# One pass over the first gate/up products, with the first product copied from bank to bank

## The chip, the cores and the metric

The kernel runs on one core of a Trainium2 chip. The core has TensorE (PE in the profile: matmuls, with the load of the stationary operand, PEld, beside them), VectorE (DVE), ScalarE (ACT), GpSimd (POOL) and SyncE (SP, which here only issues DMAs). On-chip memory is SBUF, 128 partitions wide; TensorE writes its sums to PSUM, which has eight banks of 128 x 512 float32. The metric is the device time of one execution, in microseconds, as a median of several runs. Less is better.

## The reference

One decoder layer on 2048 tokens of width 1024, all in float32:

```python
hn = rms_norm(h, mix_pre_g)
proj = hn @ w_in                                   # q, k, v and the convolution group's input u
attn_out = sliding_window_attention(q, k, v, attn_sinks, rel_bias)   # window 128
conv_out = conformer_conv(u, ...)                  # GLU, 31 taps, LayerNorm, swish, @ w_conv_pw
mixed = jnp.concatenate([attn_out, conv_out], axis=-1) @ w_out
h = h + rms_norm(mixed, mix_post_g)
hn = rms_norm(h, ffn_pre_g)
ff = (jax.nn.silu(hn @ w_gate) * (hn @ w_up)) @ w_down               # inner width 2816
h = h + rms_norm(ff, ffn_post_g)
```

## The kernel before

**Number format.** Each float32 operand of a large matmul is split into a high part (rounded to the fp32r format, a ScalarE copy) and a low part (the difference, by VectorE or GpSimd). A product takes three matmuls: high x high, high x low, low x high. One matmul covers 128 x 128 weights by 512 columns.

**Stages.** Tokens go in four tiles of 512 (t or w = 0 to 3). The letter behind the @ in a tile's name in the profile is its stage.

- A (`stage_a`): the first norm and the input projection, 14 units for each token tile. B (`stage_b`): attention in four blocks of 128 tokens. It transposes through the PSUM banks `tr` and has GpSimd mask the probabilities (line 504).
- C: the convolution. `stage_taps` does the 31 taps on VectorE; `stage_tail` (line 578) turns the result through the PSUM bank `ct`, normalises it and writes it to `mixT` in device memory.
- J (`stage_join`, lines 621 to 650): multiplies `w_conv_pw` into the lower half of `w_out` once, so that the convolution's last projection and the output projection become one. Four raw pieces of `w_out` are split into a right operand, two raw pieces of `w_pw` into left operands; the raw tile `wx` has one buffer. The results are written to `w_join`.
- W (`stage_w`, lines 714 to 762): the output projection of one token tile, from `mixT`, in four groups of two inputs; then norm and residual (`norm_w`); `hn` is written to `hn_scr` in device memory.
- H: reads columns of `hn_scr`, transposes them (`turned`, line 828) and splits them into operands of the gate/up matmuls. `stage_h_plain` (line 846) makes B11 and B21, the operands of the token tile `ws[0]`; `stage_h_sums` (line 859) makes the rest.
- F: gate and up. Two token tiles are done together, first (0, 1) and then (2, 3), with a scheme that forms a 2 x 2 block product from seven block products of sums in place of eight. A "matrix" m below is one pair of 128-wide gate or up blocks; there are 22. One block product, `product` (line 896), is 12 matmuls into one bank.
- G (`stage_p2`): the down projection by the same scheme, and the last norm (`finish`).

**The first gate/up stage.** `stage_pre` (lines 904 to 975) does two of the block products ahead of the rest, for the first 20 matrices of tiles (0, 1) and the first 16 of tiles (2, 3): A11 x B11 ("first") and A12 x B21 ("second"), which add up to one block. It runs over q: first all the first products, then all the second ones. A first product is copied by ScalarE from its bank to a `fa` tile (line 965) and written to `keeps` in device memory (line 966). For a second product that sum is read back into one of two `gb` tiles (`fetch`, line 926) and copied by ScalarE into a bank (`seed`, line 941), onto which the second product adds up. Gate results then go through Silu (line 970), up results are multiplied in, and the block is written to `mids`. `stage_p1`, which does the remaining five products of each matrix, reads `keeps` once more (line 1025, seed at line 1054). For matrices that were not done ahead it copies the first product from bank to bank itself (line 1062).

**Order of the work.** The program is written as a main sequence of generators and lanes beside it (`Lane`, lines 1297 to 1344). Each `yield` carries a cost; the main sequence advances a clock, and each lane emits work as its rate allows, if its condition holds. `until` emits the rest of a lane at once. The order of emission sets priorities, and a list scheduler with a simulated time line sets from them the final order on every engine and DMA queue. Engines work strictly in that order. The conditions that matter here:

```python
lh.add(n + ".0", stage_h_plain(ws, ops, n, off), lambda: since(lw, "W0", NH))      # B11, then B21
lw.add("W0", ..., lambda: "A3" in started and "C0" in ld.done)                     # line 1388
ld.add("J", stage_join(), lambda: "A2" in started)                                 # then C0, C1
```

**Buffers.** PSUM has four banks `mm` (products), three `tr` (attention, transposes) and one `ct`. Of the SBUF tiles named here there are four `fa`, two `gb`, eight `hl`, four `mid`, two `mb`, one `wx`, three `fc`. B11 and B21 of tiles (0, 1) lie in `x` and `hl`, those of tiles (2, 3) in `ql` and `mid`; the `mid` tiles are until then those in which the output projection of token tile 3 is summed and normalised.

Of the kernel before, what the change touches and what calls it, by code (L numbers as in the profile page):

```python
# [17 lines left out]
AF = mybir.ActivationFunctionType  # L18
# [7 lines left out]
P = 128  # L26
T = 512
# [10 lines left out]
def layer_kernel(ctx, tc, x, xT, cols, rows, sinks, relb, onehot, w_in, w_pw, w_out, w_gate, w_up, w_down, out):  # L38
    nc = tc.nc
# [7 lines left out]
    lab = ["X0"]  # L47
# [7 lines left out]
    def t_(tag, shape, dt=F32):  # L55
        return sb.tile(list(shape), dt, tag=tag, name=nm(tag), bufs=BUFS[tag])

    def f4(tag, shape=(P, D)):
        return t_(tag, shape)
# [14 lines left out]
    mm = lambda: bank("mm", 4)  # L74
    tr = lambda: bank("tr", 3)
# [517 lines left out]
    def conv_tail(t, yt):  # L593
# [14 lines left out]
        for c in range(4):  # L608
# [9 lines left out]
            yield 2  # L618
            lab[0] = L

    def stage_join():
        lab[0] = "J0"
        right = []
        for k in range(4):
            raw = f4("wx", (P, 2, T))
            nc.sync.dma_start(raw, w_out[4 + k].rearrange("p (a b) -> p a b", a=2))
            yield JL
            for n in range(2):
                lab[0] = "J0"
                right.append(split_w(raw[:, n], "mid" if k < 2 else "chl"))  # L630
            yield 1.5
            lab[0] = "J0"
        for mp in range(2):
            pair_ = t_("yt", (P, 2, 2, T), F32R)
            raw = f4("wx", (P, 2, T))
            nc.sync.dma_start(raw, w_pw[2 * mp : 2 * mp + 2].rearrange("m p t -> p m t"))
            yield JL
            lab[0] = "J0"
            left = [split_w(raw[:, m], pair_[:, m]).rearrange("p a (k c) -> p a k c", c=P) for m in range(2)]
            yield 2  # L640
            for m in range(2):
                for n in range(2):
                    lab[0] = "J0"
                    o = ct()
                    three(o, [((left[m][:, 0, k], left[m][:, 1, k]), (right[2 * k + n][:, 0], right[2 * k + n][:, 1])) for k in range(4)])
                    z = f2("fa")
                    act(z, o, AF.Copy, scale=0.5)
                    nc.scalar.dma_start(w_join[2 * mp + m, :, n * T : (n + 1) * T], z)
                    yield 4
                    lab[0] = "J0"  # L650
# [63 lines left out]
    def stage_w(w, spill, G, atag, htag, mtag, bank_of, norm=None):  # L714
        L = f"W{w}"
        lab[0] = L
        acc = [f4(atag) for _ in range(4)]

        def acts(gi, ms=None):
            aa = []  # L720
            for m in ms or load(gi):
                a = hl(htag)
                act(a[:, 0], m, AF.Copy)  # L723
                vtt(a[:, 1], m, a[:, 0].bitcast(F32), ALU.subtract)
                aa.append([a])
            return aa

        stage = t_("mb", (P, 2, T)) if w == 1 else None

        def load(gi):  # L730
            ms = []
            for c in range(G * gi, G * gi + G):
                ms.append(stage[:, c % 2] if w == 1 else f2(mtag))
                nc.sync.dma_start(ms[-1], mixT[c, :, w * T : (w + 1) * T])
            return ms

        first = load(0)
        gb = load_gb(0) if w > 1 else None
        if w != 1:
            yield 5.0 if w == 0 else 8.0  # L740
            lab[0] = L
        nxt = acts(0, first)
        for gi in range(KC // G):
            aa = nxt
            for n in range(2):
                lab[0] = L
                if n == 0 and gi + 1 < KC // G:
                    if w == 1 and G * gi + G == 4:
                        ld.until("C1")
                        lab[0] = L  # L750
                    rows_next = load(gi + 1)
                if n == 1 and gi + 1 < KC // G:
                    nxt = acts(gi + 1, rows_next)
                src = w_out[2 * gi : 2 * gi + 2] if gi < 2 else w_join[2 * gi - 4 : 2 * gi - 2]
                ws = weight(src[:, :, n * T : (n + 1) * T].rearrange("c p t -> p c t"),
                            lo_out[n, 2 * gi : 2 * gi + 2], w > 0)
                yield from block_half(acc, list(zip(aa, ws)), n, gi == 0, L, bank_of)
        tail = norm_w(w, spill, acc, mtag, gb)
        if norm:
            norm(tail)  # L760
        else:
            yield from tail
# [83 lines left out]
    def stage_h_plain(ws, ops, n, off):  # L846
        L = f"H{ws[0]}"
        for k in range(4):
            lab[0] = L
            b = turned(ws[0], k + off, tr, COLTAG[ws[0]][k] if ws[0] else "fa")  # L850
            u = f2("gb")
            act(u, b, AF.Copy, scale=g_ffn[:, k + off : k + off + 1])
            nc.scalar.dma_start(hT[ws[0] // 2][k + off], u)
            o = op_tile(ws, ops, n, k, {})
            act(o[:, 0], u, AF.Copy)
            lo(u, o, False)
            yield 2.0
# [43 lines left out]
                mat(o, w[:, a, ks], op[k][:, b], start=first and n == 0, stop=n == 11, skip_group_check=not first)  # L901
                n += 1

    def stage_pre(ws, ops, mid, keep, q0=0, q1=None):
        PRE = PRES[ws[0]]
        q1 = q1 or 2 * PRE
        L = f"F{ws[0]}"
        raws = {}
        wops = {}
        kept = {}  # L910

        def load(q):
            if q < q1 and q % 2 == 0:
                lab[0] = L
                half, m = divmod(q, PRE)
                raw = t_("raw", (P, 2, T))
                for j in range(2):
                    src, pr = MATS[m + j]
                    nc.sync.dma_start(raw[:, j], src[2 * pr][:, half * T : (half + 1) * T])
                    raws[q + j] = raw[:, j]  # L920

        def fetch(q):
            if PRE <= q <= q1:
                lab[0] = L
                kept[q] = f2("gb")
                nc.sync.dma_start(kept[q], keep[q - PRE if q < q1 else 0])

        def split(q):
            if q < q1:
                lab[0] = L  # L930
                raw = raws.pop(q)
                wops[q] = split_f(raw, hl("w"))
                lo(raw, wops[q], ws[0] and q % 2 == 1)

        seeded = {}

        def seed(q):
            if PRE <= q < q1:
                lab[0] = L
                seeded[q] = mm()  # L940
                act(seeded[q], kept.pop(q), AF.Copy)  # L941

        load(q0)
        load(q0 + 2)
        for q in range(q0, q0 + 3):
            split(q)
        for q in range(q0, q1):
            half, m = divmod(q, PRE)
            started.add(f"P{ws[0]}.{q}")
            bn = "B21" if half else "B11"  # L950
            if len(ops.get(bn, ())) < 4:
                lh.until(f"{bn}.{ws[0]}")
            split(q + 3)
            load(q + 4)
            if q + 2 == PRE:
                fetch(q + 2)
            lab[0] = L
            seed(q + 1)
            fetch(q + 3)
            lab[0] = L  # L960
            o = seeded.pop(q) if half else mm()
            product(o, wops.pop(q), ops[bn], not half)
            if not half:
                u = f2("fa")
                act(u, o, AF.Copy)
                nc.scalar.dma_start(keep[m], u)
            else:
                if MATS[m][0] is w_gate:
                    sg = f2("fa")
                    act(sg, o, AF.Silu)  # L970
                else:
                    vtt(sg, sg, o, ALU.mult)
                    nc.sync.dma_start(mid[0, MATS[m][1]], sg)
            yield 2.76
        early[ws[0]] = kept.pop(q1)

    early = {}

# [318 lines left out]
    class Lane:  # L1297
# [36 lines left out]
        def until(self, name):  # L1334
            while name not in self.done:
                assert self.items, name
                n, gen, needs = self.items[0]
                assert not needs or needs(), n
                inlane[0] = True
                for c in gen:  # L1340
                    assert c is not None
                inlane[0] = False
                self.done[n] = clk[0]
                self.items.pop(0)

# [10 lines left out]
    NS = 12  # L1356
    AHEAD = 3
    PRES = {0: 20, 2: 16}
    POOL_LO = (3, 6)
    PRE_S0, PRE_S2 = 22, 16  # L1360
    H1, H2, H3, H4 = 0, 4, 7, 11
    NH = 24
    JL = 10
    lb = Lane(RB, 0)
    lc = Lane(RC0, LC)
    lw = Lane(RW0, 0)
# [18 lines left out]
            started.add(name)  # L1385

    lb.add("X", stage_x(), lambda: "x1" in started)
    lw.add("W0", stage_w(0, True, 2, "x", "hl", "fa", mm), lambda: "A3" in started and "C0" in ld.done)
    TGA = [["hl"] * 8, ["mid"] * 4 + ["chl"] * 4, ["hl"] * 8, ["mid"] * 4 + ["hl"] * 4]
    xa = {}  # L1390
    warm = mm()
# [136 lines left out]
```

## Time and profile before

| | |
|---|---|
| median of 3 runs | 1991.51 us (1990.13 to 1993.91) |
| profiled execution | 1997.53 us, span of its instructions 1995.6 us |
| mean granted TensorE clock | 0.989 |
| PE busy | 1940.2 us (97%), 8730 matmuls |
| DVE, ACT, POOL busy | 1488.0 (75%), 970.8 (49%), 331.1 us (17%) |
| device memory | 330.08 MB read, 121.12 MB written, 226 GB/s over the span |

How to read the lines shown below: a line of the waits has the waiting engine, line and tile, what it waited for, then total us, times and longest. A line of a stretch has its bounds, its length and the busy time of PE, PEld, DVE, ACT and POOL with their counts, then the granted clock, the share of the DMA engines and GB/s. A line of a group has line, engine, operation, output and inputs, shape and count, then busy us and mean ns of one, then the idle time ahead of them by what ended it. A line of the time line has start and length in us, engine, line, operation, tiles and count; idle time before it and its releaser stand in brackets. SPq and ACTq are issues of DMAs. A DMA line has line or tiles, count, KB of each, and median us from issue to landing.

### The profile page before, as it was taken

To read this page: it belongs to the slowest core of one execution; us is meant where nothing else is said; L and a number is where in the kernel's file an instruction comes from. 1 tells how busy PE (TensorE), PEld (TensorE's weight loads), DVE (VectorE), ACT (ScalarE), POOL (GpSimd) and SP (SyncE) were. 2 spreads that over 40 slices of the span, in tenths; PEclk is the share of its full clock that TensorE was granted. 3 is DMA by queue.
4 is the path that set the end of the run, shared out by engine and by line. 5 is a ranking of instruction groups with operands and counts; after the bars stand their busy time and mean duration, and the time that the engine had idled before them with its cause. 6 is when DMAs were issued, how large, how long until landed. Compare 5 with 4: busy or idle time off the path is not lost.

```text
span 1995.6 us, 26899 instructions
## 1 busy us (share of the span) xinstructions
PE 1940.2 (97%) x8730; PEld 1546.2 (77%) x8730; DVE 1488.0 (75%) x2679; ACT 970.8 (49%) x1910; POOL 331.1 (17%) x395
## 2 busy tenths in 40 slices
PE   8999999899999999999999999999899999999998
PEld 6877677667777788878878878778688888888886
DVE  5998989955884899988759985675866665555557
ACT  5355334456566643333355446476544333345443
POOL 6001311231111300000000020003523332311000
PEclk9999999999999999999999999999999999999999
DMA  8786654567859876787477687689834442366654
GB/s 311 256 310 217 219 167 143 186 214 253 276 176 332 298 253 239 233 278 260 162 266 245 231 280 270 195 303 353 307 139 169 169 153 101 126 220 212 211 185 159
DMA packets 234364, 452.99 MB, mean 227 GB/s; under 512 B 23496, under 2 KB 49264, under 8 KB 234224
## 3 DMA queue, kind: packets, MB, share of 16 engines
q1 hardware_dynamic: 212592, 415.63, 61.8%
q10 hardware_dynamic: 19392, 28.32, 3.9%
q0 software_dynamic: 2240, 7.34, 1.0%
q8 instruction: 68, 1.11, 0.2%
q14 instruction: 72, 0.59, 0.1%
HBM read 330.08 MB, written 121.12 MB: 226 GB/s over the span
## 4 chain that ended last, share of the span: by engine, by line
PE 76%; DMA 9%; DVE 8%; issue 3%; ACT 3%; POOL 1%; SPq 0%; ACTq 0%; DVEq 0%; POOLq 0%
PE mm@F L108 30%; PE mm@G L108 18%; PE mm@A L108 14%; PE mm@W L108 4%; PE tr@W L108 4%; PE tr@B L108 3%; DMA gb@F<-keeps 2%; DVE fc@C L85 1%; PE ct@J L108 1%; DVE mid@W L85 1%; DMA mixT<-fc@C 1%; DVE w@F L85 1%; DMA chl@F<-w_up 1%; DVE fa@F L85 1%; DVE chl@F L85 1%
## 5 line engine op out<-in xcount | busy, mean ns | idle before, releaser
L85 DVE SCALAR_TENSOR_TENSOR fc@C<-glu@C,colt,fc@C 128x512 f32<-128x512 f32 x480 | 367.9, 782 | 2.4
L108 PE MATMUL mm@F<-hl@H,w@F 128*128 128x512 f32 x1056 | 254.2, 390 | 4.3 <-ACT mm@F L941 4.3
L108 PE MATMUL mm@G<-hl@G,hl@G 128*128 128x512 f32 x924 | 227.4, 397 | 7.4 <-ACT mm@G L1232 2.9
L108 PEld LDWEIGHTS mm@F<-hl@H,w@F 128*128 128x128 f32 x1056 | 197.5, 188 | 47.0 <-ACT mm@F L941 6.2
L108 PE MATMUL mm@A<-hl@A,w@A 128*128 128x512 f32 x840 | 209.4, 398 | 2.6 <-DVE hl@A L85 1.3
L108 PEld LDWEIGHTS mm@G<-hl@G,hl@G 128*128 128x128 f32 x924 | 173.5, 190 | 46.5 <-ACT mm@G L1232 3.4
L108 PE MATMUL mm@G<-w@G,hl@G 128*128 128x512 f32 x876 | 199.7, 389 | 0.0
L814 ACT ACTIVATE w@F<-chl@F 128x512 fp32r<-128x512 f32 x220 | 135.0, 624 | 118.6 <-PE mm@F L108 112.8
L108 PEld LDWEIGHTS mm@G<-w@G,hl@G 128*128 128x128 f32 x876 | 164.3, 188 | 34.4 <-issue 0.3
L108 PEld LDWEIGHTS mm@A<-hl@A,w@A 128*128 128x128 f32 x840 | 156.8, 190 | 40.6 <-DVE hl@A L85 3.0
L85 DVE TENSOR_TENSOR w@F<-chl@F,w@F 128x512 fp32r<-128x512 f32 x198 | 145.2, 735 | 39.0 <-ACT w@F L814 38.8
L108 PE MATMUL mm@F<-mid@H,w@F 128*128 128x512 f32 x528 | 132.3, 394 | 7.9 <-ACT mm@F L941 7.3
L108 PE MATMUL mm@F<-p@H,w@F 128*128 128x512 f32 x528 | 130.6, 393 | 0.0
L108 PE MATMUL mm@F<-ql@H,w@F 128*128 128x512 f32 x528 | 127.1, 390 | 2.0 <-ACT w@F L814 2.0
L108 PE MATMUL mm@F<-x@H,w@F 128*128 128x512 f32 x528 | 126.8, 391 | 1.0 <-DVE x@H L85 0.9
L108 PEld LDWEIGHTS mm@F<-mid@H,w@F 128*128 128x128 f32 x528 | 98.1, 188 | 31.4 <-ACT mm@F L941 9.6
L108 PEld LDWEIGHTS mm@F<-ql@H,w@F 128*128 128x128 f32 x528 | 98.9, 188 | 23.0 <-ACT w@F L814 2.6
L108 PEld LDWEIGHTS mm@F<-p@H,w@F 128*128 128x128 f32 x528 | 100.1, 190 | 21.3 <-ACT at@F L1068 0.4
L108 PEld LDWEIGHTS mm@F<-x@H,w@F 128*128 128x128 f32 x528 | 98.3, 188 | 23.4 <-DVE x@H L85 1.4
L108 PE MATMUL mm@W<-w@W,hl@W 128*128 128x512 f32 x384 | 106.0, 415 | 7.4 <-ACT hl@W L723 5.6
L133 ACT ACTIVATE w@A<-raw@A 128x512 fp32r<-128x512 f32 x110 | 67.4, 626 | 73.9 <-PE mm@A L108 46.1
L85 DVE TENSOR_TENSOR w@G<-raw@G,w@G 128x512 fp32r<-128x512 f32 x73 | 51.2, 701 | 67.6 <-ACT w@G L814 66.6
(301 smaller groups left out, 3307.6 us busy)
## 6 DMA issues: line engine op xcount, KB each, us to landing
mids<-fa@F SPq DMA_DIRECT2D x154, 256.0 KB, 2.7
raw@A<-w_in SPq DMA_DIRECT2D x55, 512.0 KB, 4.4
w@A<-lo_in SPq DMA_DIRECT2D x84, 256.0 KB, 3.4
fc@G<-mids SPq DMA_DIRECT2D x77, 256.0 KB, 3.3
fa@G<-mids SPq DMA_DIRECT2D x75, 256.0 KB, 4.8
gb@F<-keeps SPq DMA_DIRECT2D x74, 256.0 KB, 4.5
w@W<-lo_out SPq DMA_DIRECT2D x48, 256.0 KB, 4.2
chl@F<-w_gate SPq DMA_DIRECT2D x22, 512.0 KB, 3.9
```

What stands on the lines that cost most here:

```text
L85: r = op(*args, **kw)
L108: r = nc.tensor.matmul(*args, **kw)
L133: act(w[:, 0], raw, AF.Copy)
L814: act(w[:, 0], x, AF.Copy)
```

## The change

In `stage_pre` the order becomes pairs of matrices: m first, m+1 first, m second, m+1 second. Behind each first product, after the copy to `fa` and the write to `keeps`, which stay, ScalarE copies the bank into the next `mm` bank, and the second product adds up there. The reads of `keeps` in this stage go, but for one ahead of `stage_p1`. (The new `TWO` would leave so many matrices in the old order; it is 0 for both.) The fetch of that last one is now issued at two steps, the third and the second from the end.

The join has a second raw tile, `spare_tile()`, an `mb` tile that the output projection of token tile 1 uses later in place of its own; loads are issued two ahead, with a pause `JS` of 2 in place of `JL` of 10 behind each. W0 waits for the join in place of the convolution tail C0, and emits the rest of C0 itself ahead of its third group if that is not done. The transposes of `stage_h_plain` for token tile 0 go through `ct` in place of `tr`.

```diff
 def stage_join():
+    srcs = [w_out[4 + k].rearrange("p (a b) -> p a b", a=2) for k in range(4)]
+    srcs += [w_pw[2 * m : 2 * m + 2].rearrange("m p t -> p m t") for m in range(2)]
+    def load(i):
+        if i < len(srcs):
+            raws[i] = spare_tile() if i % 2 else f4("wx", (P, 2, T))
+            nc.sync.dma_start(raws[i], srcs[i])
+    load(0)
+    load(1)
+    yield JL
     for k in range(4):
-        raw = f4("wx", (P, 2, T))
-        nc.sync.dma_start(raw, w_out[4 + k].rearrange("p (a b) -> p a b", a=2))
-        yield JL
         for n in range(2):
-            right.append(split_w(raw[:, n], "mid" if k < 2 else "chl"))
-        yield 1.5
+            right.append(split_w(raws[k][:, n], "mid" if k < 2 else "chl"))
+        yield JS
+        load(k + 2)
+        yield JS
...
-    stage = t_("mb", (P, 2, T)) if w == 1 else None
+    stage = spare_tile() if w == 1 else None
...
-                if w == 1 and G * gi + G == 4:
-                    ld.until("C1")
+                if w < 2 and G * gi + G == 4:
+                    ld.until(f"C{w}")
...
-        b = turned(ws[0], k + off, tr, COLTAG[ws[0]][k] if ws[0] else "fa")
+        b = turned(ws[0], k + off, tr if ws[0] else ct, COLTAG[ws[0]][k] if ws[0] else "fa")
...
-def stage_pre(ws, ops, mid, keep, q0=0, q1=None):
+def stage_pre(ws, ops, mid, keep):
+    PRE, two = PRES[ws[0]], TWO[ws[0]]
+    seq = [(m, half) for half in range(2) for m in range(two)]
+    for m in range(two, PRE, 2):
+        seq += [(m + j, half) for half in range(2) for j in range(2)]
...
+    def stored(q):
+        return q == len(seq) or q < len(seq) and seq[q][1] and seq[q][0] < two
     def fetch(q):
-        if PRE <= q <= q1:
+        if stored(q):
             kept[q] = f2("gb")
-            nc.sync.dma_start(kept[q], keep[q - PRE if q < q1 else 0])
+            nc.sync.dma_start(kept[q], keep[seq[q][0] if q < len(seq) else 0])
...
-    for q in range(q0, q1):
-        half, m = divmod(q, PRE)
+    for q, (m, half) in enumerate(seq):
         bn = "B21" if half else "B11"
         if len(ops.get(bn, ())) < 4:
             lh.until(f"{bn}.{ws[0]}")
         split(q + 3)
         load(q + 4)
-        if q + 2 == PRE:
+        if stored(q + 2) and not stored(q + 1):
             fetch(q + 2)
         seed(q + 1)
         fetch(q + 3)
-        o = seeded.pop(q) if half else mm()
+        o = seeded.pop(m) if half else mm()
         product(o, wops.pop(q), ops[bn], not half)
         if not half:
             u = f2("fa")
             act(u, o, AF.Copy)
             nc.scalar.dma_start(keep[m], u)
+            if m >= two:
+                seeded[m] = mm()
+                act(seeded[m], o, AF.Copy)
...
+TWO = {0: 0, 2: 0}
-JL = 10
+JL, JS = 10, 2
...
-lw.add("W0", ..., lambda: "A3" in started and "C0" in ld.done)
+lw.add("W0", ..., lambda: "A3" in started and "J" in ld.done)
```

More of the change, by code (lines that the diff above doesn't have):

```diff
@@ L619, in conv_tail, with spare_tile @@
             lab[0] = L
+    spare = []
+    def spare_tile():
+        if not spare:
+            spare.append(t_("mb", (P, 2, T)))
+        return spare[0]
     def stage_join():
         lab[0] = "J0"
+        srcs = [w_out[4 + k].rearrange("p (a b) -> p a b", a=2) for k in range(4)]
+        srcs += [w_pw[2 * m : 2 * m + 2].rearrange("m p t -> p m t") for m in range(2)]
+        raws = {}
+        def load(i):
+            if i < len(srcs):
+                lab[0] = "J0"
+                raws[i] = spare_tile() if i % 2 else f4("wx", (P, 2, T))
[3 more added lines that the diff above has]
+        yield JL
         right = []
         for k in range(4):
-            raw = f4("wx", (P, 2, T))
-            nc.sync.dma_start(raw, w_out[4 + k].rearrange("p (a b) -> p a b", a=2))
-            yield JL
             for n in range(2):
                 lab[0] = "J0"
-                right.append(split_w(raw[:, n], "mid" if k < 2 else "chl"))
-            yield 1.5
+                right.append(split_w(raws[k][:, n], "mid" if k < 2 else "chl"))
+            yield JS
+            load(k + 2)
+            yield JS
+        for mp in range(2):
             lab[0] = "J0"
-        for mp in range(2):
             pair_ = t_("yt", (P, 2, 2, T), F32R)
[L635 to L639, printed above, removed]
+            left = [split_w(raws[4 + mp][:, m], pair_[:, m]).rearrange("p a (k c) -> p a k c", c=P) for m in range(2)]
             yield 2
@@ L902, in product @@
                 n += 1
-    def stage_pre(ws, ops, mid, keep, q0=0, q1=None):
-        PRE = PRES[ws[0]]
-        q1 = q1 or 2 * PRE
+    def stage_pre(ws, ops, mid, keep):
+        PRE, two = PRES[ws[0]], TWO[ws[0]]
         L = f"F{ws[0]}"
-        raws = {}
-        wops = {}
-        kept = {}
+        seq = [(m, half) for half in range(2) for m in range(two)]
+        for m in range(two, PRE, 2):
+            seq += [(m + j, half) for half in range(2) for j in range(2)]
+        raws, wops, kept, seeded = {}, {}, {}, {}
         def load(q):
-            if q < q1 and q % 2 == 0:
+            if q < len(seq) and q % 2 == 0:
                 lab[0] = L
-                half, m = divmod(q, PRE)
+                m, half = seq[q]
                 raw = t_("raw", (P, 2, T))
@@ L920, in load @@
                     raws[q + j] = raw[:, j]
+        def stored(q):
+            return q == len(seq) or q < len(seq) and seq[q][1] and seq[q][0] < two
         def fetch(q):
-            if PRE <= q <= q1:
+            if stored(q):
                 lab[0] = L
                 kept[q] = f2("gb")
-                nc.sync.dma_start(kept[q], keep[q - PRE if q < q1 else 0])
+                nc.sync.dma_start(kept[q], keep[seq[q][0] if q < len(seq) else 0])
         def split(q):
-            if q < q1:
+            if q < len(seq):
                 lab[0] = L
@@ L933, in split @@
                 lo(raw, wops[q], ws[0] and q % 2 == 1)
-        seeded = {}
         def seed(q):
-            if PRE <= q < q1:
+            if q < len(seq) and stored(q):
                 lab[0] = L
[L940 to L945, printed above, removed]
+                seeded[seq[q][0]] = mm()
+                act(seeded[seq[q][0]], kept.pop(q), AF.Copy)
+        load(0)
+        load(2)
+        for q in range(3):
             split(q)
-        for q in range(q0, q1):
-            half, m = divmod(q, PRE)
+        for q, (m, half) in enumerate(seq):
             started.add(f"P{ws[0]}.{q}")
@@ L954, in stage_pre @@
             load(q + 4)
-            if q + 2 == PRE:
+            if stored(q + 2) and not stored(q + 1):
                 fetch(q + 2)
-            lab[0] = L
             seed(q + 1)
@@ L974, in stage_pre @@
             yield 2.76
-        early[ws[0]] = kept.pop(q1)
+        early[ws[0]] = kept.pop(len(seq))
     early = {}
@@ L1338, in until @@
                 assert not needs or needs(), n
+                was = inlane[0]
                 inlane[0] = True
@@ L1341, in until @@
                     assert c is not None
-                inlane[0] = False
+                inlane[0] = was
                 self.done[n] = clk[0]
@@ L1387, in layer_kernel @@
     lb.add("X", stage_x(), lambda: "x1" in started)
-    lw.add("W0", stage_w(0, True, 2, "x", "hl", "fa", mm), lambda: "A3" in started and "C0" in ld.done)
+    lw.add("W0", stage_w(0, True, 2, "x", "hl", "fa", mm), lambda: "A3" in started and "J" in ld.done)
     TGA = [["hl"] * 8, ["mid"] * 4 + ["chl"] * 4, ["hl"] * 8, ["mid"] * 4 + ["hl"] * 4]
```

## The prediction

> **What bounds the kernel now.** I read the page first (busy times, then the chain that ended last), then the waits of TensorE, then the busy times by stretch.
>
> ```profile
> span 1995.6 us, 26899 instructions
> PE 1940.2 (97%) x8730; PEld 1546.2 (77%) x8730; DVE 1488.0 (75%) x2679; ACT 970.8 (49%) x1910; POOL 331.1 (17%) x395
> ...
> PE 76%; DMA 9%; DVE 8%; issue 3%; ACT 3%; POOL 1%; SPq 0%; ACTq 0%; DVEq 0%; POOLq 0%
> ```
>
> TensorE is the bound: 1995.6 - 1940.2 leaves 55.4 us in which it is idle. No matmul is removed or added, so the change can only act on those 55.4 us. The waits of TensorE say whose they are (columns: total us, times, longest):
>
> ```profile
> PE mm@F L108 <- ACT mm@F L941: 11.5, 11, 2.8
> PE mm@W L108 <- ACT hl@W L723: 5.6, 3, 3.9
> PE tr@B L108 <- POOL p@B L504: 4.4, 1, 4.4
> ```
>
> The largest is for line 941, the ScalarE copy that seeds a bank with a first product read back from memory. The stretches (length, then busy us of PE, PEld, DVE, ACT, POOL, clock, DMA share) are: end of the second output projection, the two halves of the first gate/up stage, the two halves of the second.
>
> ```profile
> 501.00:569.00 68.00, 68.00 (x311) 47.76 (x310) 56.20 (x148) 37.55 (x99) 6.81 (x16) 0.95 0.68 225
> 569.00:629.00 60.00, 59.04 (x285) 44.57 (x284) 42.27 (x85) 36.91 (x79) 9.09 (x16) 1.00 0.82 279
> 629.00:700.00 71.00, 65.67 (x299) 52.63 (x298) 47.67 (x68) 50.66 (x89) 20.25 (x24) 1.00 0.87 298
> 1343.00:1387.00 44.00, 44.00 (x198) 36.41 (x197) 25.36 (x60) 27.68 (x59) 14.81 (x19) 1.00 0.98 348
> 1387.00:1441.00 54.00, 45.94 (x211) 35.88 (x210) 45.35 (x54) 33.78 (x61) 28.61 (x18) 1.00 0.93 324
> ```
>
> The first halves are full; the seeded second halves lose 71.00 - 65.67 = 5.3 and 54.00 - 45.94 = 8.1 us. The clock is full in all four, so this is waiting. What ScalarE waits for over the whole run:
>
> ```profile
> ACT mm@F L941 <- DMA gb@F<-keeps: 21.4, 15, 4.0
> ...
> gb@F<-keeps SPq DMA_DIRECT2D x74, 256.0 KB, 4.5
> keeps<-fa@F ACTq DMA_DIRECT2D x36, 256.0 KB, 5.3
> ```
>
> The seed is late because its tile is late: two `gb` tiles, each refilled only after its seed was copied, and 4.5 us to land.
>
> **The change part by part.**
>
> **One pass.** Removed: 36 reads of 256 KB (9.4 MB where the DMA engines are 0.82 to 0.98 busy), their issues on SP's queue, and 36 copies from SBUF into a bank. Added: 36 copies from bank to bank. The trace has that copy, at line 1062 of the next stage:
>
> ```profile
> L965 ACT ACTIVATE fa@F<-mm@F 128x512 f32<-128x512 f32 x36 | 21.0, 590 | 12.7 <-DVE mid@W L85 5.0 <-DMA h_scr<-mid@W 3.0 <-PE mm@F L108 2.3
> L941 ACT ACTIVATE mm@F<-gb@F 128x512 f32<-128x512 f32 x36 | 21.4, 597 | 23.3 <-DMA gb@F<-keeps 21.4 <-DMA out<-x@G 1.0 <-DMA wx@G<-h_scr 0.9
> L1062 ACT ACTIVATE mm@F<-mm@F 128x512 f32<-128x512 f32 x8 | 4.7, 582 | 12.2 <-PE mm@F L108 12.2
> ```
>
> 36 x (597 - 582) ns is 0.5 us of ScalarE time, nothing. What counts is the due time. The order becomes m first, m+1 first, m second, m+1 second, so a seed is due one product after its source ends. A product is 12 matmuls; this row gives 25.55 / 112 = 0.228 us each, 2.74 us a product:
>
> ```profile
> 1343.49 6.87 PE L108 MATMUL mm@F<-ql@H,w@F 128*128 128x512 f32 x29
> 1349.75 25.55 PE L108 MATMUL mm@F<-ql@H,w@F 128*128 128x512 f32 x112
> ```
>
> On ScalarE stand the copy to `fa` (0.590) and the seed (0.582): 1.17 us, so some 1.5 us of slack. Line 1062 has the same slack, one product, and no row of TensorE's waits names it in 8 uses. So the 11.5 us should go. What stays is a ScalarE that is blocked in order, now in front of a seed:
>
> ```profile
> ACT w@F L814 <- DMA raw@F<-w_gate: 3.2, 2, 2.1
> ACT mid@H L887 <- DVE chl@H L85: 2.1, 1, 2.1
> ...
> ACT hl@H L887 <- DVE chl@H L85: 3.8, 1, 3.8
> ```
>
> (The first two from the stretch 629 to 700, the third from 1387 to 1441.) Beyond the slack these are 0.6, 0.6 and 2.3 us; with the wait for a free `fa` tile in the first half (5.0 us in the row of line 965, some 3.5 beyond the slack, hidden before by the four banks), 7.0 us if each meets a seed. A seed follows every second product, so I take half, +3.5; the ends are 0 and +11.5 (as many waits as now). The four banks suffice: the first bank of a pair has had its last reader two products (5.5 us) before it is taken again. The write of each product to `keeps` stays and nobody waits for it before the next stage. The first sum for the next stage is now fetched twice (4.5 us, in place of nothing); both land under the last two products, and if they did not, one seed would be up to 4.5 us late.
>
> **The second operand becomes due early.** The third product, not the 21st or 17th, needs B21. First stage:
>
> ```profile
> 529.17 1.92 SPq L810 DMA_DIRECT2D fa@H<-hn_scr  x2
> 493.23 0.60 PE L611 MATMUL ct@C<-ident,yt@C 128*128 128x128 f32 x4
> 561.25 0.60 PE L832 MATMUL tr@H<-ident,fa@H 128*128 128x128 f32 x4
> 575.64 3.00 PE L108 MATMUL mm@F<-x@H,w@F 128*128 128x512 f32 x12 [0.94 <-DVE x@H L85]
> 579.48 1.19 PE L108 MATMUL mm@F<-x@H,w@F 128*128 128x512 f32 x4
> 583.36 0.68 DVE L85 TENSOR_TENSOR hl@H<-gb@H,hl@H 128x512 fp32r<-128x512 f32 x1
> 596.12 0.69 DVE L85 TENSOR_TENSOR hl@H<-gb@H,hl@H 128x512 fp32r<-128x512 f32 x1 [0.57 <-ACT hl@H L855]
> ```
>
> Before, the four B21 columns are ready between 584.0 and 596.8, the third product starts at 579.5. But the loads of the first four columns were issued by 531 and their first transpose ran at 561: 30 us in which they stood in line for a `tr` bank behind the attention. Now they take `ct`, free after 493.8. Eight columns pass through two `gb` tiles, each held through a write to memory: with the 5.3 us of such a write and 0.6 to fill it, about 3 us a column, an estimate; 8 x 3 from 531 is 555, some 24 us ahead of need. I take 0, and -0.9 for the wait for `x@H`, which has the same cause. If the cover goes, see the first rival. The eight transposes cost TensorE the same wherever they run, and the engine is full there (68.00 of 68.00).
>
> Second stage: B21 lies in the tiles that the last normalisation holds until it is written out.
>
> ```profile
> 1351.17 0.69 DVE L85 TENSOR_TENSOR mid@H<-gb@H,mid@H 128x512 fp32r<-128x512 f32 x1
> ```
>
> Its last column is ready at 1351.9; the third product, 24 x 0.228 after 1343.5, starts at 1349.0 and needs the fourth column 9 matmuls later, at 1351.0: +0.9. Nothing speeds this up; ends 0 and +3.
>
> **Silu beside Exp.** Silu now starts with the third product, about 583, instead of 644:
>
> ```profile
> 642.88 1.28 ACT L970 ACT_TABLE_LOAD   x1
> 584.30 0.39 ACT L479 ACTIVATE p@B<-p@B,sm@B 128x128 f32<-128x128 f32 x1
> 587.09 0.39 ACT L479 ACTIVATE p@B<-p@B,sm@B 128x128 f32<-128x128 f32 x1
> ```
>
> The last Exps of the attention run at 584.3 to 587.5. If a Silu falls before them, two table loads of 1.28 us are added in front of seeds with 1.5 us of slack: I take +0.8, ends 0 and +2.6.
>
> The Trainium skill's ScalarE: Activation LUTs, section What ACT_TABLE_LOAD costs, speaks against the change here: a switch between table sets costs about 2.66 us with the drain, so two more would be 5.3 us of ScalarE, and the sum below would be up to 2.7 us worse. The trace agrees on the load (1.28 against 1.283 us) and shows no row for a drain.
>
> **Joining and first projection.** In the lane's costs, loads for the join become one wait of 10 and then 4 a pair: 10 + 16 + 36 = 62 in place of 46 + 56 = 102, with two raw tiles. What that meets:
>
> ```profile
> 207.58 1.15 ACT L133 ACTIVATE chl@J<-wx@J 128x512 fp32r<-128x512 f32 x2 [4.81 <-DMA wx@J<-w_out]
> 208.29 6.76 POOL L135 TENSOR_TENSOR chl@J<-wx@J,chl@J 128x512 fp32r<-128x512 f32 x2 [5.09 <-ACT chl@J L133]
> 424.57 0.73 PE L108 MATMUL mm@W<-w@W,hl@W 128*128 128x512 f32 x2 [1.02 <-ACT hl@W L723]
> 431.23 3.06 PE L108 MATMUL mm@W<-w@W,hl@W 128*128 128x512 f32 x12 [0.65 <-ACT hl@W L723]
> ```
>
> The second tile takes away ScalarE's waits for the raw load, but GpSimd's subtractions, 3.38 us each here, come closer together, ahead of the attention's masks: TensorE's one wait of 4.4 us for them may go (-4.4) or come again (+4.4 each); nearest to the row, I take 0. An earlier join lets the first convolution tail start earlier, so the projection's third group of inputs, which comes from it, is earlier: the waits of 1.02 and 0.65 go, -1.7. The spare tile, shared with the second projection, is read last by the join some 100 us before that needs it: 0.
>
> **The sum**: -11.5 + 3.5 + 0.9 + 0.8 - 0.9 - 1.7 = -8.9 us. The profiled execution took 1997.53 us (span 1995.6), the median of the runs is 1991.51, 0.3% less; scaled, 1991.5 - 8.9 = 1982.6.
>
> **The rivals.**
>
> First, on the other side: B21 comes late in the first stage. Were the columns ready when they are now, the third product, ending at 582.2 by its start, would end no sooner than 596.8 + 0.7: 15.3 us late. That gives 1982.6 + 15.3 = 1997.9; with the two products of the next pair run ahead (5.5 us), 1992.4. It decides from a delay of about 13 us. For it: ScalarE and VectorE are busy in that stretch (37.55 and 56.20 of 68). Against: the 24 us above.
>
> Second, GpSimd: all eight right-hand subtractions close together, 27 us at 3.38 us, and each of the four attention blocks beside the join waits 4.4 us: three more waits, +13.2, giving 1995.8. From three on it is slower. Against: beside all four blocks TensorE waited for a mask once (the 1 in its row).
>
> Third, no change: ScalarE is as late with seeds as the DMA was. Then +11.5 stands in place of +3.5: 1990.6. For it: ScalarE is busy 50.66 of 71.00. Against: line 1062.
>
> Fourth, a larger gain: the waits of 4.4 and 3.9 us of attention and projection go as well, and no residue is left: -8.9 - 4.4 - 3.9 - 3.5 = -20.7, giving 1970.8.
>
> **How the numbers follow.** A measurement of this kernel tells about 0.2%, 4 us, from no change. The forecast (1977 to 1987) gets 0.42, the larger gain 0.15, no change 0.13, late B21 0.20, GpSimd 0.10. So faster 0.57, same 0.13, slower 0.30. The range runs from 1971 (the larger gain) to 1999 (late B21 with a table load).
>
> **What would show it.** No row of line 926 but the last fetches; the new copy at about 582 ns, 36 times; TensorE's idle time in the two gate/up stages below 5 us in place of 13.4; `tr@H` of the first stage before 560 on `ct`; two to four table loads. A TensorE wait for `hl@H` of many microseconds, or more waits for `p@B` between 200 and 330, would make it wrong. Since the order on every engine is planned anew, waits of a few microseconds can also appear elsewhere; I know no row to price those.

## The result and the profile after

The changed kernel takes 1982.54 us as a median, the kernel before 1989.8 us, both over 22 executions. The ratio is 0.9968 with a 95% interval of 0.9958 to 0.9978: 0.32%, some 6 us, faster. The profiled execution took 1986.73 us, its span is 1984.7 us. Executions of one kernel lie 13 to 18 us apart, and the profiled one of the kernel before (1997.53 us) is slower than all 22, so two profiles alone don't show a difference of a few microseconds; one that returns in several traces does.

The head of its page and the waits of TensorE:

```profile
span 1984.7 us, 26851 instructions
...
PE 1937.4 (98%) x8730; PEld 1545.6 (78%) x8730; DVE 1493.7 (75%) x2679; ACT 969.5 (49%) x1910; POOL 335.2 (17%) x395
...
HBM read 320.64 MB, written 121.12 MB: 223 GB/s over the span
```

```profile
PE mm@F L108 <- ACT mm@F L1071: 3.7, 2, 2.4
PE mm@F L108 <- ACT mm@F L983: 3.5, 3, 1.9
PE mm@F L108 <- ACT w@F L829: 3.5, 1, 3.5
PE tr@B L108 <- DVE sm@B L460: 2.8, 3, 2.0
...
PE tr@B L108 <- POOL p@B L504: 0.2, 1, 0.2
```

TensorE's idle time fell from 55.4 to 47.3 us. There are 36 reads fewer (9.4 MB less read), and the seed, now line 983, is waited for 3 times and 3.5 us in place of 11 times and 11.5 us. But in the five-product stage behind it three waits are larger: line 1071 has 3.7 us where its counterpart of before had none listed, lines 829 and 1092 have 3.5 and 2.6 us where theirs (814 and 1075) had 2.0 and 0.6. By stretches, before and after (end of the projection for tokens 0 to 1023; first gate/up stage; the five-product stage behind it; second gate/up stage):

```profile
501.30:568.80 67.50, 67.50 (x310) 47.30 (x308) 55.70 (x147) 37.05 (x98) 6.81 (x16) 0.95 0.68 223
568.80:701.70 132.90, 126.61 (x591) 98.82 (x589) 91.85 (x156) 89.33 (x171) 29.34 (x40) 1.00 0.84 286
701.70:1015.80 314.10, 310.89 (x1362) 255.58 (x1362) 267.75 (x431) 119.34 (x216) 0.00 (x0) 0.99 0.71 238
1343.50:1444.50 101.00, 92.94 (x420) 74.77 (x417) 71.11 (x114) 62.60 (x121) 44.49 (x38) 1.00 0.95 331
```

```profile
497.00:569.30 72.30, 71.50 (x370) 50.73 (x368) 55.84 (x160) 45.08 (x110) 10.20 (x17) 0.98 0.70 235
569.30:694.10 124.80, 121.29 (x542) 97.69 (x541) 83.06 (x127) 81.45 (x155) 27.75 (x38) 0.99 0.71 242
694.10:1014.70 320.60, 310.60 (x1350) 253.68 (x1349) 264.98 (x427) 118.07 (x214) 0.00 (x0) 0.99 0.68 229
1340.30:1433.40 93.10, 91.48 (x419) 75.23 (x418) 78.11 (x114) 61.69 (x120) 46.04 (x38) 1.00 0.93 314
```

The second gate/up stage is 7.9 us shorter with the same work (420 and 419 matmuls listed), and its idle time fell from 8.1 to 1.6 us. The lengths of the first one don't compare, since 49 matmuls fewer stand in it (some now run ahead of it); its idle time fell from 6.3 to 3.5 us. It ends 7.6 us earlier (694.1 against 701.7), but by 1014.7 only 1.1 us of that are left: in the five-product stage the idle time grew from 3.2 to 10.0 us.

### The profile page after: what moved, and what is told of

The parts are those of the page before. It is cut to its first block, busy times and chain, and to the rows that moved or that the text cites. A ratio compares the mean times of both kernels' runs of the same rounds, so it can differ in the third digit from the quotient of the medians.

```text
span 1984.7 us, 26851 instructions
## 1 busy us (share of the span) xinstructions
PE 1937.4 (98%) x8730; PEld 1545.6 (78%) x8730; DVE 1493.7 (75%) x2679; ACT 969.5 (49%) x1910; POOL 335.2 (17%) x395
## 4 chain that ended last, share of the span: by engine, by line
PE 77%; DVE 8%; DMA 8%; ACT 3%; issue 2%; POOL 1%; SPq 0%; ACTq 0%; DVEq 0%; POOLq 0%
PE mm@F L108 36%; PE mm@G L108 16%; PE mm@A L108 12%; PE mm@W L108 4%; PE tr@W L108 3%; PE tr@B L108 3%; DVE fc@C L85 3%; PE ct@J L108 1%; DMA raw@A<-w_in 1%; DVE mid@W L85 1%; DMA at@W<-mixT 1%; DMA gb@F<-keeps 1%; DMA mids<-fa@F 1%; DVE w@F L85 1%; DMA mixT<-fc@C 1%
## 5 line engine op out<-in xcount | busy, mean ns | idle before, releaser
L108 PE MATMUL mm@F<-ql@H,w@F 128*128 128x512 f32 x528 | 131.3, 392 | 7.2 <-ACT mm@F L1071 3.7
```

What stands on the lines that cost most here:

```text
L108: r = nc.tensor.matmul(*args, **kw)
```

## The experiments

My theory was that seeds waiting for memory were the loss, and that their removal in both stages was the gain. The rivals were that the other parts made the gain, and that the first stage's share was lost again.

**The other parts without one pass (e1_old_order).**

```diff
-TWO = {0: 0, 2: 0}
+TWO = {0: 20, 2: 16}
```

> The changed kernel with its join, first projection and transposes, but with the gate/up products in the old order (all first products, then all second ones, seeds read back from memory). Theory A, the gain comes from seeds that no longer wait for memory: 1988 to 1991 us where before takes 1990, TensorE idle about 13 us in the two gate/up stages as before. Rival B, the gain comes from the other parts or from the newly planned order: about 1983 us (ratio 0.997).

Ratio 0.9969 (0.9951 to 0.9987). The theory falls in this form: join, projection and transposes alone give as much as the whole change.

**One pass in one stage only (e5_first_only, e6_second_only)**, with the other parts of the change.

```diff
-TWO = {0: 0, 2: 0}
+TWO = {0: 0, 2: 16}     # e5_first_only
+TWO = {0: 20, 2: 0}     # e6_second_only
```

> One pass for tiles (0, 1) only, the old order for tiles (2, 3). Theory A: some 3 to 5 us of the 7, so 1985 to 1987 us. Rival C, what the first stage gains is given back in the five-product stage behind it (there TensorE's waits grew from 3.2 to 9.9 us between the two profiles): 1989 to 1991 us, ratio 1.000.

> One pass for tiles (2, 3) only, the old order for tiles (0, 1). Theory A: 1983 to 1986 us, the 8.1 us of waits at the end of the second stage go. Rival C: the whole gain, 1982 to 1984 us, ratio 0.996 to 0.997. Rival B: about 1983 us as well, but with the waits of the second stage still there.

First only: 0.9984 (0.997 to 0.9998). Second only: 0.9938 (0.9919 to 0.9957), 12 us faster than before, and its interval does not meet that of the changed kernel. So one pass helps in the second stage and seems to cost in the first: from the second alone to both it loses 0.3%, from the old order (e1) to the first alone 0.15%, the latter inside the intervals.

**Second stage alone (e14_second_alone).** The kernel before with `TWO = {0: 20, 2: 0}`, all else as it was.

> The kernel before with one edit: tiles (2, 3) in one pass. Join, first projection, transposes and tiles (0, 1) as before. Theory A2, the second stage's gain is that of the seeds and stands by itself: the stretch from its first product to the next stage shrinks from 101 to 93 us, the ratio is 0.996 to 0.997. Rival B2, it is an effect of the new plan as a whole: no change, and the seeds' waits of 8 us still there in another form.

Ratio 0.9965 (0.9949 to 0.998). Its second stage:

```profile
1339.00:1432.10 93.10, 91.33 (x419) 75.23 (x417) 78.89 (x114) 62.22 (x123) 46.16 (x38) 1.00 0.93 312
```

and the only wait of TensorE that is listed in this stretch:

```profile
PE tr@H L839 <- issue: 1.8, 1, 1.8
```

93.1 in place of 101.0 us, and no wait for a seed is left. Here the theory holds, with one edit. The stage's length returns in other traces: it is 92.6 to 93.2 us in all eight kernels with one pass and one copy of each seed, and 100.1 to 101.9 us in four of the five with the old order there (before, e1, e5, e16). The fifth comes next.

**The join alone and ct alone (e15_join_alone, e16_ct_alone).** Products in the old order in both; the first has the new join and W0's condition, the second only this:

```diff
-            b = turned(ws[0], k + off, tr, ...)
+            b = turned(ws[0], k + off, tr if ws[0] else ct, ...)
```

> The kernel before with the new join alone (second raw tile, shorter pauses, W0's condition); products in the old order, transposes through tr. Run e1, which has ct as well, gained 6 us. If that is the join's: 1983 to 1986 us, ratio 0.996 to 0.998, with the attention's last block ending earlier than at 610. If it is ct's: 1.000.

> The kernel before with the transposes of B11 and B21 of tiles (0, 1) through ct alone; join and products in the old form. If ct makes the 6 us of run e1: ratio 0.996 to 0.998, and the seeds of the first stage in time. If the join does: 1.000.

Join 0.9997 (0.9983 to 1.0012), ct 0.997 (0.9954 to 0.9986). The trace of the join alone has the second gate/up stage, in the old order, at

```profile
1352.30:1444.80 92.50, 91.22 (x415) 74.73 (x414) 62.80 (x105) 59.44 (x114) 39.67 (x38) 1.00 0.95 332
```

That is as short as with one pass, though every seed is read from memory; the first stage loses 0.4 us only. So a seed read from memory need not be late: in the other plans it was, in this one it wasn't. Yet the kernel was no faster. Its idle time stands elsewhere: 7.5 us in the five-product stage (3.2 before), 14.4 us between that and the second gate/up stage (10.1 before). An edit is worth what the whole plan makes of it.

The 6 us of the other parts are those of the bank. W0's condition does nothing: with the old one in its place beside the new join, the planned program is the same on every engine. The largest wait of TensorE in the first gate/up stage with ct alone, for the seed (line 949 there):

```profile
PE mm@F L108 <- ACT mm@F L949: 1.6, 2, 1.0
```

In the old order, with seeds still read from memory, the waits for them there fall from 4.3 to 1.6 us. So ct takes away much of the wait that one pass was to take away in that stage. These 2.7 us are less than half of its 6; where the rest comes from is not shown.

**The change without the new join (e3_old_join), and without ct (e2_tr).**

```diff
-            b = turned(ws[0], k + off, tr if ws[0] else ct, ...)     # e2_tr
+            b = turned(ws[0], k + off, tr, ...)
```

> The changed kernel with the join and the first projection of the kernel before; one pass in both stages and ct kept. If the join makes the 6 us of run e1: 1988 to 1992 us, ratio 0.999 to 1.001. If it does not: as the changed kernel, ratio 0.997.

> The changed kernel with the transposes of B11 and B21 of tiles (0, 1) on the tr banks as before. If the early due time of B21 is what ct pays for: the first product with B21 waits 10 to 15 us for hl@H, 1993 to 1998 us (ratio 1.002 to 1.004). If the planner fills the time with other products, or the bank does not matter: 1982 to 1984 us.

Old join 0.9955 (0.9939 to 0.9971), tr 0.996 (0.9939 to 0.998): neither part is needed when the other is there. With tr and the new join, the columns of B21 were ready in time (the last in the second line, at 572.4), and TensorE paid for the bank with a wait of its own:

```profile
563.62 0.68 DVE L85 TENSOR_TENSOR hl@H<-gb@H,hl@H 128x512 fp32r<-128x512 f32 x1
571.42 0.96 DVE L85 TENSOR_TENSOR hl@H<-gb@H,hl@H 128x512 fp32r<-128x512 f32 x1
```

```profile
552.30 0.82 PE L847 MATMUL tr@H<-ident,fa@H 128*128 128x128 f32 x4 [3.61 <-ACT gb@H L867]
```

**One pass in both stages, and nothing else (e17_one_pass_alone).**

> The kernel before with one pass in both stages and nothing else: old join, transposes of B11 and B21 through tr. Here the early due time of B21 has no help. By the rival of the late B21 (columns ready at 584 to 597 as before): TensorE waits 10 to 15 us for hl@H near 580, ratio 1.000 to 1.003, although the second stage still saves 7 us. If the planner brings B21 forward by itself: 0.995 to 0.997.

Ratio 1.0016 (1.0003 to 1.0029): slower than before, although its second stage is as short as in the changed kernel (the profile has 92.7 us). By the ratios that is some 10 us over the second stage alone; the two profiles are 5.6 us apart. Its columns and the wait in the first stage:

```profile
575.64 0.69 DVE L85 TENSOR_TENSOR x@H<-gb@H,x@H 128x512 fp32r<-128x512 f32 x1
591.19 0.73 DVE L85 TENSOR_TENSOR hl@H<-gb@H,hl@H 128x512 fp32r<-128x512 f32 x1 [0.31 <-ACT hl@H L862]
```

```profile
572.88 1.65 PE L108 MATMUL mm@F<-x@H,w@F 128*128 128x512 f32 x3 [3.55 <-DVE x@H L85]
583.89 0.66 PE L839 MATMUL tr@H<-ident,fa@H 128*128 128x128 f32 x4 [1.06 <-ACT gb@H L859]
584.85 0.96 PE L108 MATMUL mm@F<-hl@H,w@F 128*128 128x512 f32 x3 [0.30 <-ACT mm@F L975]
```

The time is that of the rival of the late B21, its mechanism isn't seen. The columns come at 580 to 592, but the plan puts other products and the attention before them, and TensorE waits 3.6 us for B11 and little for B21. The first gate/up stage ends at 701.3 us here and at 700.5 with the second stage alone; 4.1 of the 5.6 us between the two profiles come behind it, in the five-product stage (318.7 against 314.6 us). So the trace does not show what makes this kernel slower than the kernel before. What the runs do show is that the same edit gives 0.996 with either part beside it, and that the last column of B21 is then ready earlier: at 579.9 with ct and the old join, at 572.4 with tr and the new one, at 591.9 here. That this is the reason is likely, not shown.

**Two edits together (e13_second_old_join).** The kernel before with ct and with one pass in the second stage.

> The kernel before with two edits: one pass for tiles (2, 3) and ct. If the two effects (0.9965 and 0.9970 alone) are independent: 0.9935, 1979 to 1981 us, faster than the changed kernel. If they take the same idle time: 0.9965.

Ratio 0.9942 (0.9927 to 0.9958), median 1978.42 us. The two effects add up: 0.9965 x 0.9970 = 0.9935 lies in the interval. This kernel and the one with the new join as well (0.9938) beat the kernel before, and the changed one by intervals that just touch or just miss; they can't be told from each other.

**Does the first stage lose by the crowd on ScalarE (e18_eight)?** As the last kernel, but from the ninth matrix on the first stage goes in one pass too:

```diff
-TWO = {0: 20, 2: 0}
+TWO = {0: 8, 2: 0}
```

> As the run with one pass for (2, 3) and ct, but in the first stage the matrices from the ninth on go in one pass too (the first eight in the old order), so that no seed from bank to bank falls among the last Exps of the attention. If one pass costs in the first stage because of that crowd on ScalarE: as that run or up to 2 us faster. If it costs by itself: 2 to 5 us slower than that run.

Ratio 0.9966 (0.9953 to 0.9978), 0.24% more than the kernel with 20; the intervals overlap a little. That speaks against the crowd of the last Exps on ScalarE as the only cause, and settles nothing. Its two long waits:

```profile
599.83 8.97 PE L108 MATMUL mm@F<-hl@H,w@F 128*128 128x512 f32 x31 [2.20 <-ACT mm@F L949]
685.88 4.61 PE L108 MATMUL mm@F<-x@H,w@F 128*128 128x512 f32 x12 [2.75 <-DVE fa@F L85]
```

The first is a seed read from memory, at the turn from the eight first products to the eight second ones; the other comes near the end. Neither is a seed from bank to bank, so this run says something of a mixed order and not why a full one costs.

**How much room a seed has (e11_second_four).** The kernel of e6_second_only, each seed copied four times:

```diff
-                    act(seeded[m], o, AF.Copy)
+                    for _ in range(4):
+                        act(seeded[m], o, AF.Copy)
```

> The changed join and ct, one pass for (2, 3) only, and each seed copied four times over in place of once: 3 x 0.58 us more of ScalarE for each of 16 seeds. With a slack of 1.5 us behind a seed, 2.3 us of copies plus the 0.6 to fa make it 0.2 us late and more where ScalarE has other work: the second stage takes 97 to 105 us in place of 93, 3 to 12 us slower than the same kernel with one copy. If seeds have far more slack than that: 93 us still.

Ratio 1.0015 (1.0001 to 1.0029), some 15 us over the same kernel with one copy. Its second stage, and TensorE's waits there:

```profile
1324.10:1432.60 108.50, 95.62 (x408) 77.00 (x406) 69.91 (x114) 83.48 (x165) 39.41 (x37) 0.92 0.77 260
```

```profile
PE tr@H L847 <- issue: 6.8, 1, 6.8
PE tr@H L847 <- DMA fc@H<-hn_scr: 3.7, 1, 3.7
PE mm@F L108 <- ACT mm@F L984: 2.5, 2, 2.3
```

108.5 in place of 93.0 us, more than the 97 to 105 expected; but the stage starts some 10 us earlier than in the kernel with one copy (1324.1 against 1334.4), so its length isn't all loss. More ScalarE time behind a seed made the kernel slower, but mostly not by late seeds (2.5 us): the plan itself moved, and the longest waits stand at transposes. So the run does not measure the slack of a seed.

## Why the prediction was right or wrong

The forecast of 1982.6 us, its sign and its range held; 8.9 us were forecast and some 6 to 7 measured. That 1982.6 meets 1982.54 is luck: it starts from a median of three runs (1991.5), where 22 give 1989.8. And the sum came out by terms that were wrong in both directions.

- **Seeds, -11.5 and +3.5.** Right in the second stage: a seed takes 595 ns there and 589 in the first, TensorE never waits for it in the second, and one pass alone is worth 0.35%, 7 us, of the 7.3 us of waits that this stage had. The step that failed is the other part, "So the 11.5 us should go", for the first stage. There one pass doesn't gain: beside ct it costs 0.1 to 0.3% (0.9942 to 0.9955 with the old join, inside the intervals; 0.9938 to 0.9968 with the new one), without ct and join 0.5%. All four pairs point the same way, and only the one without ct and join is far beyond its intervals. Much of the first stage's wait for seeds was taken by ct in the old order already. The residue of 3.5 us that I took is what line 983 shows, 3.5 us. Its kind was right, a ScalarE busy in order ahead of a seed, and its size is luck: the 5.0 us that I read as one wait for a `fa` tile were two, 3.40 and 1.56 us at 606 and 609, so that 2.0 and not 3.5 us lay beyond the slack, and the 2.3 us that I priced in the second stage did not come.
- **B21 in the first stage, 0 and -0.9.** The mechanism was right. The columns passed through `ct` from 525 on and the last was ready at 567.3, where I had estimated 555; the wait for `x@H` went:

```profile
524.96 0.33 PE L847 MATMUL ct@H<-ident,fa@H 128*128 128x128 f32 x1
566.64 0.68 DVE L85 TENSOR_TENSOR hl@H<-gb@H,hl@H 128x512 fp32r<-128x512 f32 x1
```

The size was wrong: ct by itself is worth 0.3%, 6 us, where I gave 0.9. I had priced it only as the cover for B21 and the wait for `x@H`.
- **B21 in the second stage, +0.9.** It cost nothing; no wait for `mid@H` is listed.
- **Silu beside Exp, +0.8.** There was one table load, as before, at 579.0 in place of 642.9, behind the last Exp. The crowd cost something else. The first seed stood behind four squares of the norm and the last Exps, and TensorE waited 1.9 us:

```profile
575.48 0.39 ACT L479 ACTIVATE p@B<-p@B,sm@B 128x128 f32<-128x128 f32 x1
576.34 0.58 ACT L983 ACTIVATE mm@F<-mm@F 128x512 f32<-128x512 f32 x1
579.00 1.28 ACT L987 ACT_TABLE_LOAD   x1
```

```profile
576.97 4.61 PE L108 MATMUL mm@F<-hl@H,w@F 128*128 128x512 f32 x12 [1.92 <-ACT mm@F L983]
```

- **Join and first projection, -1.7.** Worth nothing alone (0.9997). The waits of the projection for `hl@W` (5.6 us) are not listed any more, and the wait of 4.4 us for GpSimd did go, as the fourth rival had it; others came in their place (2.8 us for `sm@B` among them). Ahead of the first gate/up stage TensorE idles 18.3 us before and 13.2 in the changed kernel, but 19.2 with the join alone, where the transposes on tr wait 4.4 us for `gb@H`: without ct the join gives back there what it saves.
- **The rivals.** A time as the late B21 would give came only without ct and join (1.0016), and without its long wait for `hl@H`. No one rival alone came true in the change.
- **The sign that I named.** TensorE's idle time in the two gate/up stages was to fall from 13.4 to below 5 us. It fell to 5.1. With the join alone it is 1.7, and that kernel is no faster: idle time in two stages does not tell the gain.
- **What no step had.** TensorE idles 6.8 us longer in the five-product stage. It waits there for its own seeds (line 1071) and for ScalarE's splits behind them. ScalarE had itself stood still before these seeds, for 9.24 us until the read from `keeps` had landed and for 8.74 us until VectorE was done:

```profile
874.28 0.60 ACT L1071 ACTIVATE mm@F<-gb@F 128x512 f32<-128x512 f32 x1 [9.24 <-DMA gb@F<-keeps]
875.49 1.22 PE L108 MATMUL mm@F<-ql@H,w@F 128*128 128x512 f32 x2 [3.50 <-ACT w@F L829]
843.88 0.60 ACT L1071 ACTIVATE mm@F<-gb@F 128x512 f32<-128x512 f32 x1 [8.74 <-DVE w@F L85]
844.53 1.65 PE L108 MATMUL mm@F<-ql@H,w@F 128*128 128x512 f32 x6 [2.39 <-ACT mm@F L1071]
```

No code of that stage was changed, but its order was planned anew. That it idles longer is seen in several runs, to different amounts, and one pass in the first stage isn't needed for it: 6.7 and 7.9 us in e1 and e6, where that stage has the old order. Why is not settled. Nor is settled why one pass costs in the first stage once B21 is in time; the run with eight matrices speaks against the Exps as the only cause.

## What to carry to other kernels

When an edit comes with helpers, run each of them alone and each pair: here a change of bank, brought along as a cover, was worth nearly as much as the edit, and two cures for the same wait need not add up. When an edit makes an operand due earlier, look for what would make it ready earlier: the same edit was 0.2% slower than before without such a part and 0.4% faster with either of two. Read a stage's gain where the next one starts: 7.6 us were there at the end of the first stage and 1.1 at the end of the next. And where a planner sets every order, look for a plan without your edit that lacks the wait as well: the join alone had both gate/up stages full and gained nothing.

## What the runs showed of the hardware

After a short wait of TensorE its matmuls are slower in some places. In the changed kernel, 12 matmuls took 4.61 us after a wait of 1.92, where 12 take 2.9 to 3.0 elsewhere, and the granted clock over 569 to 590 was 0.92. With 2.75 us of wait in e18_eight it was 4.61 as well. In e11_second_four the clock over the whole second stage was 0.92, in the same kernel with one copy 1.00; that stage has 11.0 us more idle time and is 15.5 us longer, though 11 matmuls fewer are listed in it. It is no rule: before, a wait of 2.84 us was followed by 12 matmuls in 3.04:

```profile
1422.21 3.04 PE L108 MATMUL mm@F<-mid@H,w@F 128*128 128x512 f32 x12 [2.84 <-ACT mm@F L941]
```

The Trainium skill's TensorE: Matmul & The Clock Gate, Part 1, has the clock halve after an idle window of about 3.4 us. The waits of 1.92 and 2.75 us are shorter than that, and were followed by slower matmuls all the same; no run shows where the bound lies.
